# State products of the prompt in fp32r: three passes over high and low parts, two pairs of heads side by side, first in each block

## The chip, the core and the metric

The kernel runs on one core of one Trainium2 chip. The metric is the device time of one execution, in microseconds. A core has a matmul engine (PE, with its weight loads as PEld), a vector engine (DVE), a scalar engine (ACT), a general engine (POOL) and a queue engine (SP, written SPq in the profile), each of which runs its own list of instructions in order and waits on semaphores of the others. SP issues nearly all loads, POOL the stores of results.

## What is computed

One layer of a streaming trunk for two requests at once: a prompt of 256 frames, and 8 running streams of 16 frames, 384 tokens in all (`T`; `TP` = 256 is the prompt's part). A combined projection of 2048 inputs feeds a pooling branch, a state-space branch with 64 heads of 64 channels in 8 groups, and gates; a second norm, a squared-ReLU MLP and residual sums follow. What the change touches is the state at the end of the prompt, the term behind the plus here:

```python
    last = cum[:, -1]
    w_end = jnp.exp(last[:, None] - cum)
    h = h * jnp.exp(last)[..., None, None] + jnp.einsum('bsgn,bsgr,bsgrp->bgrpn', Bc, w_end, xdt)
```

For the prompt h begins at zero, so over all 256 tokens the final state of a head is a sum over tokens of B (128 columns, one B for the 8 heads of a group) times the decayed input of the head (64 columns). It is an output, `new_ssm_prompt`; nothing else of this layer reads it. Two heads make a pair of 128 columns; a group has four pairs, and a block of the kernel treats two.

The group's gated norm, which the prediction comes to, is

```python
    h = y.astype(jnp.float32) * jax.nn.silu(z.astype(jnp.float32))
    h = h * lax.rsqrt(jnp.mean(h * h, axis=-1, keepdims=True) + EPS)
```

with the mean over the 512 channels of a group.

## The kernel before

Every large product is done in three passes: an fp32 operand is split into a high part in the format fp32r (a copy on ACT, L77, named `wh`) and a low part (a subtraction on DVE, L78, named `wl`), and `mm3` (L161) adds high x high, high x low and low x high. A **unit** is half a weight column of the input projection, 8 x 3 = 24 matmuls of 128 x 128 by 128 x 384; two units (q 0 and q 1) give one projection. `flow` (L121) runs a list of units: it fetches weights four units ahead on SP, splits them three units ahead, runs the unit's matmuls, calls its post-processing, and then lets `work` drain deferred tasks.

Deferred tasks are closures in the deque `todo` with a cost written by hand. `later(cost, tag, f)` adds one at the end; `work(2.6)` after each unit takes tasks until their costs have used up the allowance, with a debt carried on; `need(tag)` takes all tasks up to that tag at once. The order in which instructions stand on ACT and DVE follows from this: nothing is reordered behind it.

The stretch from 480 to 1310 us holds eight groups, g = 0 to 7. Each runs the projections BT and CT (B and C of the group), x0 to x3 and z0 to z3, and up to g = 6 one gate. The x projections pass a short causal conv with SiLU (`conv_units`, L522 on; its task goes to the front of the deque); z has a SiLU (L563). Between them stand, by a list written out by hand:

- `block(old, new)` (L587) twice per group: after x2 with old = (g-1, 1) and new = (g, 0), and after z3 with old = (g, 0) and new = (g, 1). Per block and for `old`, PE makes Y (L598 on; the decayed attention-like product, from the tiles `E` and `xdt`), closes it with the contribution of the running streams (L627), and makes the state products `pp` (L631); for `new` it transposes x (L638) into `xdt` and `xdw` (the input times its decay to the end of the prompt), and in a group's first block also B (L643) and C x B (`cb`, L646). `pp` is copied on ACT to `pe` (L662) and stored by two POOL DMAs.
- A block queues, for `new`: `xhl` (high and low part of the running streams' part of `xdw`, L718 and L719, stored to `x_scr` by SP at L720), the exponentials of four heads in two `E` tiles with their powers (L762 to L771), the decay of the running states `hs` (L703, on DVE) and the masks on E (L782); and for `old` the gated products: y x silu(z) (L729), its square on ACT (L732, L735), the running sum `ssum` (L738), and after the fourth the sum's high part `sh` (ACT, L744) and low part `sl` (DVE, L745).
- `update` (L841): the state update of the running streams, 8 fp32r matmuls of 128 x 256, once after z1's first unit for (g, 0) and once within x0 of the next group.
- `norm_mm(g-1)` (L786): after z1's second unit, two matmuls with a matrix of ones, `bc_g`, that sum `sh` (L790) and `sl` (L791) of group g-1 over partitions. So there is one each in g = 1 to 7, ahead of z2's first unit, and a last one between the gates.

In PSUM, 2 banks hold the projections (`mmtile`) and 6 in rotation everything else (`sstile`).

Of the kernel before, what the change touches and what calls it, by code (L numbers as in the profile page):

```python
# [7 lines left out]
F32 = mybir.dt.float32  # L8
# [7 lines left out]
P = 128  # L16
# [20 lines left out]
def build(ctx, tc, io):  # L37
# [190 lines left out]
    rstd = small.tile([P, T], F32, name="rstd")  # L228
    cst2 = small.tile([P, C_END - C_MASK], F32, name="cst2")

# [70 lines left out]
    with tc.manual_schedule():  # L301
        v.memset(warm, 0.0)
        s.dma_start(gpre, io["vec"][:, V_GPRE : V_GPRE + 16])
        for kind, *a in sum(pieces, []):
            (xload if kind == "x" else oload)(*a)
        sy.dma_start(vec, io["vec"])
        sy.dma_start(pst, io["state_pool"])
        sy.dma_start(cst[:, :C_MASK], io["cst"][:, :C_MASK])
        sy.dma_start(cst2, io["cst"][:, C_MASK:])
# [21 lines left out]
    small.tile([P, 88], F32, name="pad_small")  # L331
    tok = small.tile([P, 11, NH], F32, name="tok")
    decb = small.tile([P, NH, NB], F32, name="decb")
    with tc.tile_pool(name="phc", bufs=1, reuse_waits="tile") as pc, tc.tile_pool(name="phc2", bufs=2, reuse_waits="tile") as pc2:
        bufs = []
        for i in range(2):
# [78 lines left out]
        def dt_phase(pb):  # L415
# [22 lines left out]
            v.tensor_scalar(dta, dt, nA, -1.0, ALU.mult, ALU.mult)  # L438
            v.tensor_tensor_scan(cum, cst2[:NH, C_SCAN - C_MASK : C_SCAN - C_MASK + T], dta, 0.0, ALU.mult, ALU.add)
            sy.dma_start(cum_scr, cum)  # L440
# [62 lines left out]
    s.activation(onesr, ones, AF.Copy)  # L503
    nrm = pd1.tile([P, 32], F32, name="nrm")
    v.tensor_scalar(nrm, vec[:, V_NRM : V_NRM + 32], -1.0 / 8192.0, None, ALU.mult)
    pd1.tile([P, 64], F32, name="pad_phd")
    seg = lambda a: a.rearrange("p (b t) -> p b t", b=24)
    ncv = [0]

# [38 lines left out]
    def gate_units(n):  # L548
        def post(ps):
            t = small.tile([P, T], F32, tag="gbt", name=f"gbt{n}", bufs=2)  # L550
# [27 lines left out]
    def make_Cm(g):  # L578
# [6 lines left out]
        )  # L585

    def block(old, new):  # L587
        Y = []
        if old:
            g, hf = old  # L590
            need(f"E{g}_{hf * 2}", f"E{g}_{hf * 2 + 1}")
            d = S[g]
            for j in (hf * 2, hf * 2 + 1):
                y = sstile(f"Y{g}_{j}")
                Y.append(y)
                for sb, e0, c0, n in ((0, 0, 0, TP), (1, TP, P, P), (2, T, TP, P)):
# [28 lines left out]
        if old:  # L625
            for y, j2 in zip(Y, range(2)):
                te.matmul(y[:, TP:T], d["yis"][hf][:, j2 * P : j2 * P + P], ident, start=False, stop=True, skip_group_check=True)  # L627
            pp = sstile(f"pp{g}_{hf}")
            for j2 in range(2):
                for b in range(2):  # L630
                    te.matmul(pp[:, j2 * P : j2 * P + P], d["xdw"][hf][:, j2, b, :], d["Bk"][:, b, :], start=b == 0, stop=b == 1)  # L631
        trx = []
# [79 lines left out]
    def state_tasks(g, hf):  # L712
        d = S[g]

        def parts():
            xhl = pd.tile([P, 2, 2, P], F32R, tag="xhl", name=f"xhl{g}_{hf}", bufs=1)
            x = d["xdw"][hf][:, :, 2, :]
            s.activation(xhl[:, 0], x, AF.Copy)  # L718
            v.tensor_tensor(xhl[:, 1], x, xhl[:, 0].bitcast(F32), ALU.subtract)  # L719
            sy.dma_start(x_scr[g * 2 + hf], xhl.bitcast(F32))  # L720

        later(0.5, f"xhl{g}_{hf}", parts)

# [62 lines left out]
    def norm_mm(g):  # L786
# [4 lines left out]
        te.matmul(bc, onesr, d["sl"], start=False, stop=True)  # L791
        ms = pd.tile([P, T], F32, tag="ms", name=f"ms_g{g}", bufs=1)
        y = pd.tile([P, T], F32, tag="ssum", name=f"nwy_g{g}", bufs=1)
# [109 lines left out]

    ab, ms_, held = [], [], {}
    AR = 7
# [36 lines left out]
    at(narrow)  # L942
    items += tail_[5:8]
    at(norm_mm, G - 1)
# [760 lines left out]
```

## Time and profile before

| | |
|---|---|
| Time, median of 3 runs (lowest to highest) | 2799.66 us (2799.36 to 2801.17) |
| The profiled execution: its own time | 2798.04 us |
| The profiled execution: span of the core | 2796.3 us |
| Granted PE clock, mean over the span | 0.999 |
| PE busy | 2783.0 us, 100% |
| DVE busy | 1766.5 us, 63% |
| ACT busy | 1323.6 us, 47% |
| POOL busy | 191.0 us, 7% |
| HBM | 412.35 MB read, 77.89 MB written, 175 GB/s |
| State products L631: PE busy, instructions | 17.0 us, 128 |
| Table loads on ACT at L540, L762 and L552 | 16, 16 and 8, 1283 ns each |

A row of a timeline reads: start in us from the span's start, duration in us, engine, line, operation, output <- inputs, shape, count; in brackets the engine's idle time before it and what ended it. Rows with a count over 1 stand for so many instructions in a row, with the time from the first's start to the last's end. A matmul's time is modelled and overlaps the next one's, so PE's durations don't add up; the distance from start to start does.

### The profile page before, as it was taken

How to read it: one execution, taken by the hardware profiler on the slowest of the kernel's cores; microseconds unless marked ns; L12 is line 12 of the kernel's file. 1: busy time of each engine (PE TensorE's matmuls, PEld its weight loads, DVE VectorE, ACT ScalarE, POOL GpSimd, SP SyncE). 2: the span in 40 equal slices, each digit the busy share in tenths (PEclk: the TensorE clock that was granted, in tenths of full speed). 3: DMA queues.
4: the chain of work that ended last, by engine and by line, in shares of the span. 5: the costliest groups of instructions: out<-in, count | busy, mean ns of one | idle time of the engine just before them, and what ended most of it. 6: DMA issues, size and time to landing. Idle time of an engine off the chain costs nothing.

```text
span 2796.3 us, 40260 instructions
## 1 busy us (share of the span) xinstructions
PE 2783.0 (100%) x15964; PEld 2653.5 (95%) x15964; DVE 1766.5 (63%) x2217; ACT 1323.6 (47%) x2076; POOL 191.0 (7%) x295
## 2 busy tenths in 40 slices
PE   9999999999999999999999999999999999999998
PEld 9999999999999999999999988999999999999997
DVE  8774334567767667677643334666767667676766
ACT  6443223555555555554422223545555555555553
POOL 0000000000000000001000000000111111111111
PEclk9999999999999999999999999999999999999999
DMA  6444445556556556555744454445666666666656
GB/s 223 135 133 138 140 137 175 183 178 215 193 182 211 196 184 206 201 183 185 263 156 157 147 203 133 155 166 184 179 160 166 162 163 162 178 176 186 183 127 246
DMA packets 161468, 492.89 MB, mean 176 GB/s; under 512 B 20032, under 2 KB 43392, under 8 KB 156416
## 3 DMA queue, kind: packets, MB, share of 16 engines
q1 hardware_dynamic: 133008, 406.07, 43.4%
q0 software_dynamic: 28128, 84.24, 12.7%
q8 instruction: 125, 2.05, 0.3%
q14 instruction: 63, 0.52, 0.1%
q10 hardware_dynamic: 144, 0.01, 0.0%
HBM read 412.35 MB, written 77.89 MB: 175 GB/s over the span
## 4 chain that ended last, share of the span: by engine, by line
PE 98%; DVE 1%; ACT 0%; SPq 0%; issue 0%; DMA 0%; DVEq 0%; ACTq 0%
PE pj_up L162 6%; PE pj_up L164 6%; PE pj_up L163 6%; PE pj_x L163 5%; PE pj_x L164 5%; PE pj_x L162 5%; PE wd L1405 3%; PE pj_sp L162 3%; PE pj_z L164 3%; PE wd L1407 3%; PE wd L1406 3%; PE pj_z L163 3%; PE pj_z L162 3%; PE pj_sp L163 3%; PE pj_sp L164 3%; PE t L1405 2%
## 5 line engine op out<-in xcount | busy, mean ns | idle before, releaser
L162 PE MATMUL pj_up<-x1h,wh_up 128*128 128x384 f32 x992 | 334.2, 337 | 0.0
L163 PE MATMUL pj_up<-x1l,wh_up 128*128 128x384 f32 x992 | 333.3, 336 | 0.0
L164 PE MATMUL pj_up<-x1h,wl_up 128*128 128x384 f32 x992 | 333.3, 336 | 0.0
L162 PE MATMUL pj_x<-xgh,wh_x 128*128 128x384 f32 x768 | 257.2, 335 | 0.0
L164 PE MATMUL pj_x<-xgh,wl_x 128*128 128x384 f32 x768 | 256.6, 334 | 0.0
L163 PE MATMUL pj_x<-xgl,wh_x 128*128 128x384 f32 x768 | 256.6, 334 | 0.0
L78 DVE TENSOR_TENSOR wl_wd<-raw,wh_wd 128x1024 fp32r<-128x1024 f32 x168 | 201.8, 1223 | 62.8 <-ACT wh_wd L77 61.2
L77 ACT ACTIVATE wh_wd<-raw 128x1024 fp32r<-128x1024 f32 x168 | 174.2, 1053 | 84.5 <-PE pj_up L163 42.1
L162 PEld LDWEIGHTS pj_up<-x1h,wh_up 128*128 128x128 f32 x992 | 186.5, 188 | 4.5
L163 PEld LDWEIGHTS pj_up<-x1l,wh_up 128*128 128x128 f32 x992 | 186.5, 188 | 4.5
L164 PEld LDWEIGHTS pj_up<-x1h,wl_up 128*128 128x128 f32 x992 | 186.5, 188 | 0.0
L164 PE MATMUL pj_z<-xgh,wl_z 128*128 128x384 f32 x512 | 171.1, 334 | 0.0
L162 PE MATMUL pj_z<-xgh,wh_z 128*128 128x384 f32 x512 | 171.1, 334 | 0.0
L163 PE MATMUL pj_z<-xgl,wh_z 128*128 128x384 f32 x512 | 171.1, 334 | 0.0
L164 PE MATMUL pj_sp<-abh,wl_sp 128*128 128x384 f32 x512 | 171.0, 334 | 0.0
L163 PE MATMUL pj_sp<-abl,wh_sp 128*128 128x384 f32 x512 | 171.0, 334 | 0.0
L162 PE MATMUL pj_sp<-abh,wh_sp 128*128 128x384 f32 x512 | 171.0, 334 | 0.0
L78 DVE TENSOR_TENSOR wl_sp<-w_sp,wh_sp 128x1024 fp32r<-128x1024 f32 x64 | 78.4, 1225 | 110.0 <-ACT wh_sp L77 110.0
L162 PEld LDWEIGHTS pj_x<-xgh,wh_x 128*128 128x128 f32 x768 | 144.2, 188 | 0.0
L163 PEld LDWEIGHTS pj_x<-xgl,wh_x 128*128 128x128 f32 x768 | 144.2, 188 | 0.0
L164 PEld LDWEIGHTS pj_x<-xgh,wl_x 128*128 128x128 f32 x768 | 144.2, 188 | 0.0
L78 DVE TENSOR_TENSOR wl_x<-w_x,wh_x 128x1024 fp32r<-128x1024 f32 x72 | 87.4, 1221 | 81.4 <-ACT wh_x L77 81.4
(388 smaller groups left out, 7085.2 us busy)
## 6 DMA issues: line engine op xcount, KB each, us to landing
w_up<-w_up SPq DMA_DIRECT2D x126, 512.0 KB, 4.5
raw<-w_down SPq DMA_DIRECT2D x112, 512.0 KB, 7.2
w_x<-w_in SPq DMA_DIRECT2D x96, 512.0 KB, 4.2
w_z<-w_in SPq DMA_DIRECT2D x64, 512.0 KB, 4.4
w_sp<-w_ssd SPq DMA_DIRECT2D x64, 512.0 KB, 4.7
acc_scr<-ev POOLq DMA_DIRECT2D x126, 256.0 KB, 4.4
w_ga<-w_in SPq DMA_DIRECT2D x32, 512.0 KB, 3.5
w_pp<-w_pp SPq DMA_DIRECT2D x32, 512.0 KB, 3.4
```

The source lines that it names most:

```text
L77: s.activation(h, w, AF.Copy)
L78: v.tensor_tensor(l, w, h.bitcast(F32), ALU.subtract)
L162: te.matmul(out, wh, xh, start=first, stop=False)
L163: te.matmul(out, wh, xl, start=False, stop=False)
L164: return te.matmul(out, wl, xh, start=False, stop=last)
L1405: te.matmul(o, ah, wh[:, c], start=first, stop=False)
L1406: te.matmul(o, ah, wl[:, c], start=False, stop=False)
L1407: te.matmul(o, al, wh[:, c], start=False, stop=fin)
```

## The change

- The prompt's state products use fp32r: per block six matmuls (three passes for each of two token blocks of 128) in place of eight fp32 instructions. The operands are exchanged: B is now stationary and `xdw` moves, both pairs of heads side by side, so 256 columns at a time. The result is the state transposed, and the host's reordering of the output follows.
- For this B is split into high and low part for all three token blocks (one ACT copy and one DVE subtraction of 128 x 384 per group), and `xhl` holds all three blocks of `xdw` (ACT and DVE 128 x 768 in place of 128 x 256). Its task is charged 1.0 instead of 0.5, and `x_scr` is written by two SP DMAs.
- A block with a successor makes the state products first, ahead of Y. Those of the very last block come after a gate unit in the tail, directly ahead of the last `norm_mm`.
- The copy out (`state_out`) goes through the buffer `gbt`, and one POOL DMA stores 256 columns.
- Around it, small tiles move: the scan's ones get a tile and a POOL load of their own, `nrm` moves to another pool, the tiles `ms` and `cacc` share a buffer.

```diff
+    def state(g, hf):
+        need(f"xhl{g}_{hf}")
+        d = S[g]
+        pp = sstile(f"pp{g}_{hf}")
+        for b in range(2):
+            bh, bl = (d["Bk"][:, i, b, :] for i in range(2))
+            xh, xl = (d["xhl"][0][:, i, :, b, :] for i in range(2))
+            mm3(pp[:, : 2 * P].rearrange("p (j q) -> p j q", j=2), bh, bl, xh, xl, b == 0, b == 1)
+        return pp
+
+    def state_out(g, hf, pp):
+        pe = small.tile([P, T], F32, tag="gbt", name=f"pe{g}_{hf}", bufs=1)[:, : 2 * P]
+        s.copy(pe, pp[:, : 2 * P])
+        gp.dma_start(io["new_ssm_p"][g * 2 + hf], pe)
...
             need(f"E{g}_{hf * 2}", f"E{g}_{hf * 2 + 1}")
             d = S[g]
+            if new:
+                pp = state(g, hf)
             for j in (hf * 2, hf * 2 + 1):
...
-            pp = sstile(f"pp{g}_{hf}")
-            for j2 in range(2):
-                for b in range(2):
-                    te.matmul(pp[:, j2 * P : j2 * P + P], d["xdw"][hf][:, j2, b, :], d["Bk"][:, b, :], start=b == 0, stop=b == 1)
...
-            pe = pd.tile([P, 2 * P], F32, tag="pe", name=f"pe{g}_{hf}", bufs=1)
-            s.copy(pe, pp[:, : 2 * P])
-            for j2 in range(2):
-                gp.dma_start(io["new_ssm_p"][g * 4 + hf * 2 + j2], pe[:, j2 * P : j2 * P + P])
+            if new:
+                state_out(g, hf, pp)
...
-                Bk = d2["Bk"] = pd.tile([P, 2, P], F32, tag="Bk", name=f"Bk{g2}", bufs=1)
-                s.copy(Bk.rearrange("p b n -> p (b n)"), trB[:, :TP])
-                Bhl = pd.tile([P, 2, P], F32R, tag="Bhl", name=f"Bhl{g2}", bufs=1)
-                s.activation(Bhl[:, 0, :], trB[:, TP:T], AF.Copy)
-                v.tensor_tensor(Bhl[:, 1, :], trB[:, TP:T], Bhl[:, 0, :].bitcast(F32), ALU.subtract)
-                sy.dma_start(b_scr[g2], Bhl.bitcast(F32))
+                Bk = d2["Bk"] = pd.tile([P, 2, 3, P], F32R, tag="Bk", name=f"Bk{g2}", bufs=1)
+                tb = trB[:, :T].rearrange("p (b n) -> p b n", b=3)
+                s.activation(Bk[:, 0], tb, AF.Copy)
+                v.tensor_tensor(Bk[:, 1], tb, Bk[:, 0].bitcast(F32), ALU.subtract)
+                sy.dma_start(b_scr[g2], Bk[:, :, 2, :].bitcast(F32))
...
-        def parts():
-            xhl = pd.tile([P, 2, 2, P], F32R, tag="xhl", name=f"xhl{g}_{hf}", bufs=1)
-            x = d["xdw"][hf][:, :, 2, :]
-            s.activation(xhl[:, 0], x, AF.Copy)
-            v.tensor_tensor(xhl[:, 1], x, xhl[:, 0].bitcast(F32), ALU.subtract)
-            sy.dma_start(x_scr[g * 2 + hf], xhl.bitcast(F32))
-
-        later(0.5, f"xhl{g}_{hf}", parts)
+        def parts(b):
+            if "xhl" not in d or d["xhl"][1] != hf:
+                d["xhl"] = pd.tile([P, 2, 2, 3, P], F32R, tag="xhl", name=f"xhl{g}_{hf}", bufs=1), hf
+            xhl = d["xhl"][0]
+            x = d["xdw"][hf][:, :, b, :]
+            s.activation(xhl[:, 0, :, b, :], x, AF.Copy)
+            v.tensor_tensor(xhl[:, 1, :, b, :], x, xhl[:, 0, :, b, :].bitcast(F32), ALU.subtract)
+            if b.stop == 3:
+                for i in range(2):
+                    sy.dma_start(x_scr[g * 2 + hf][:, i], xhl[:, i, :, 2, :].bitcast(F32))
+
+        if (g, hf) != (G - 1, 1):
+            later(1.0, f"xhl{g}_{hf}", lambda: parts(slice(0, 3)))
+            return
+        later(0.5, f"xhl{g}_{hf}", lambda: parts(slice(2, 3)))
+        held["parts"] = lambda: parts(slice(0, 2))
...
-    items += tail_[5:8]
+    items += tail_[5:7]
+    at(lambda: held["parts"]())
+    items += tail_[7:8]
+    at(lambda: state_out(G - 1, 1, state(G - 1, 1)))
     at(norm_mm, G - 1)
```

Three places of the instruction lists show what moves. The first is PE in the first block of group 1, from the last matmul of x2 on: state products `pp`, `Y`, the running streams' product `yi`, and the transposes `trx`. Before:

```order
L164 MATMUL pj_x_5586<-xgh_401,wl_x_1_5537 128x384
L598 MATMUL Y_2_5656<-E_2_5203,xdt_2_5160 64x256 x2
L598 MATMUL Y_2_5656<-E_2_5203,xdt_2_5160 64x128 x4
L598 MATMUL Y_3_5663<-E_3_5214,xdt_3_5163 64x256 x2
L598 MATMUL Y_3_5663<-E_3_5214,xdt_3_5163 64x128 x4
L618 MATMUL yi_0_5670<-hs_0_5166,Cm_5417 32x128 x16
L627 MATMUL Y_2_5656<-cst,yis_1_5151 128x128
L627 MATMUL Y_3_5663<-cst,yis_1_5151 128x128
L631 MATMUL pp_1_5689<-Bk_4704,xdw_1_5159 128x128 x4
L638 MATMUL trx_0_5694<-cst,xs_5501 128x128 x3
```

After:

```order
L164 MATMUL pj_x_5589<-xgh_401,wl_x_1_5540 128x384
L162 MATMUL pp_1_5659<-xhl_1_5201,Bk_4706 128x256
L163 MATMUL pp_1_5659<-xhl_1_5201,Bk_4706 128x256
L164 MATMUL pp_1_5659<-xhl_1_5201,Bk_4706 128x256
L162 MATMUL pp_1_5659<-xhl_1_5201,Bk_4706 128x256
L163 MATMUL pp_1_5659<-xhl_1_5201,Bk_4706 128x256
L164 MATMUL pp_1_5659<-xhl_1_5201,Bk_4706 128x256
L620 MATMUL Y_2_5666<-E_2_5206,xdt_2_5162 64x256 x2
L620 MATMUL Y_2_5666<-E_2_5206,xdt_2_5162 64x128 x4
L620 MATMUL Y_3_5673<-E_3_5217,xdt_3_5165 64x256 x2
```

The products moved ahead of Y, to the end of the unit before the block.

The second is ACT behind that block, from the powers of the second E tile (before) or the unit split that took their place (after), up to the split of z2's first unit; `xs` is the conv's SiLU and `ysq` a square of the gated norm. Before:

```order
L770 ACTIVATE E_1_5779<-E_1_5779 128x2x128
L771 ACTIVATE E_1_5779<-E_1_5779 128x2x256
L77 ACTIVATE wh_z_1_0_5818<-w_z_1_0_5733 128x1024
L526 COPY cbuf_4238<-cstate 128x8x3
L528 COPY cbuf_4238<-cbuf_4238 128x15x3
L531 ACTIVATE cacc_5825<-cbuf_4238,vec 128x384
L532 COPY cstate<-cbuf_4238 128x27
L540 ACT_TABLE_LOAD
L540 ACTIVATE xs_5831<-cacc_5825,vec 128x384
L77 ACTIVATE wh_z_1_1_5874<-w_z_1_1_5792 128x1024
L735 ACTIVATE ysq_2_5880<-zs_2_5034 128x384
L77 ACTIVATE wh_z_2_0_5908<-w_z_2_0_5847 128x1024
```

After:

```order
L77 ACTIVATE wh_z_1_0_5815<-w_z_1_0_5735 128x1024
L528 COPY cbuf_4241<-cstate 128x8x3
L530 COPY cbuf_4241<-cbuf_4241 128x15x3
L533 ACTIVATE cacc_5822<-cbuf_4241,vec 128x384
L534 COPY cstate<-cbuf_4241 128x27
L542 ACT_TABLE_LOAD
L542 ACTIVATE xs_5828<-cacc_5822,vec 128x384
L785 ACT_TABLE_LOAD
L785 ACTIVATE E_1_5782<-cbc_1_5510,tok 128x128
L787 ACTIVATE E_1_5782<-cbc_1_5510,tok 128x128 x3
L793 ACTIVATE E_1_5782<-E_1_5782 128x2x128
L77 ACTIVATE wh_z_1_1_5876<-w_z_1_1_5789 128x1024
```

The second head of E_1 and the powers moved behind the SiLU, with a table load of their own; in the whole list there are 70 table loads where there were 47.

The third is DVE in the same group, from the decay of hs (before) or the split that passed it (after) to the low part `sl`. Before:

```order
L703 TENSOR_TENSOR hs_0_5166<-hs_0_5166,decb 128x2048
L78 TENSOR_TENSOR wl_z_1_1_5875<-w_z_1_1_5792,wh_z_1_1_5874 128x1024
L738 TENSOR_TENSOR ssum_5292<-ssum_5292,ysq_1_5295 128x384
L729 TENSOR_TENSOR zs_2_5034<-zs_2_5034,xs_4660 128x384
L78 TENSOR_TENSOR wl_z_2_0_5909<-w_z_2_0_5847,wh_z_2_0_5908 128x1024
L562 TENSOR_TENSOR zs_0_5912<-pj_z_0_5849,rstd 128x384
L738 TENSOR_TENSOR ssum_5292<-ssum_5292,ysq_2_5880 128x384
L729 TENSOR_TENSOR zs_3_5102<-zs_3_5102,xs_4810 128x384
L738 TENSOR_TENSOR ssum_5292<-ssum_5292,ysq_3_5917 128x384
L745 TENSOR_TENSOR sl_5921<-ssum_5292,sh_5920 128x384
```

After:

```order
L78 TENSOR_TENSOR wl_z_1_1_5877<-w_z_1_1_5789,wh_z_1_1_5876 128x1024
L718 TENSOR_TENSOR hs_0_5168<-hs_0_5168,decb 128x2048
L78 TENSOR_TENSOR wl_z_2_0_5908<-w_z_2_0_5849,wh_z_2_0_5907 128x1024
L567 TENSOR_TENSOR zs_0_5911<-pj_z_0_5851,rstd 128x384
L761 TENSOR_TENSOR ssum_5295<-ssum_5295,ysq_1_5298 128x384
L752 TENSOR_TENSOR zs_2_5035<-zs_2_5035,xs_4662 128x384
L761 TENSOR_TENSOR ssum_5295<-ssum_5295,ysq_2_5916 128x384
L752 TENSOR_TENSOR zs_3_5103<-zs_3_5103,xs_4805 128x384
L761 TENSOR_TENSOR ssum_5295<-ssum_5295,ysq_3_5920 128x384
L768 TENSOR_TENSOR sl_5924<-ssum_5295,sh_5923 128x384
```

The decay moved behind the split wl_z_1_1, and the third gated product with the sum ahead of it behind the split wl_z_2_0 and zs_0. On PE, the matmuls `bc_g` that read sh and sl stand where they stood, between z1's second unit and z2's first.

More of the change, by code (lines that the diff above doesn't have):

```diff
@@ L228, in build @@
     rstd = small.tile([P, T], F32, name="rstd")
-    cst2 = small.tile([P, C_END - C_MASK], F32, name="cst2")
+    cst2 = small.tile([P, C_SCAN - C_MASK], F32, name="cst2")
     xg, xr = [None] * KD, [None] * KD
@@ L308, in build @@
         sy.dma_start(cst[:, :C_MASK], io["cst"][:, :C_MASK])
-        sy.dma_start(cst2, io["cst"][:, C_MASK:])
+        sy.dma_start(cst2, io["cst"][:, C_MASK:C_SCAN])
         f4 = [wfetch(win[5, q], f"p4_{q}") for q in range(2)]
@@ L329, in build @@
     pha.close()
-    small.tile([P, 88], F32, name="pad_small")
+    small.tile([P, 80], F32, name="pad_small")
+    nrm = small.tile([P, 32], F32, name="nrm")
     tok = small.tile([P, 11, NH], F32, name="tok")
@@ L334, in build @@
     with tc.tile_pool(name="phc", bufs=1, reuse_waits="tile") as pc, tc.tile_pool(name="phc2", bufs=2, reuse_waits="tile") as pc2:
+        scan = pc.tile([NH, T], F32, name="scan")
+        gp.dma_start(scan, io["cst"][:NH, C_SCAN : C_SCAN + T])
         bufs = []
@@ L438, in dt_phase @@
             v.tensor_scalar(dta, dt, nA, -1.0, ALU.mult, ALU.mult)
-            v.tensor_tensor_scan(cum, cst2[:NH, C_SCAN - C_MASK : C_SCAN - C_MASK + T], dta, 0.0, ALU.mult, ALU.add)
+            v.tensor_tensor_scan(cum, scan, dta, 0.0, ALU.mult, ALU.add)
             sy.dma_start(cum_scr, cum)
@@ L503, in build @@
     s.activation(onesr, ones, AF.Copy)
-    nrm = pd1.tile([P, 32], F32, name="nrm")
     v.tensor_scalar(nrm, vec[:, V_NRM : V_NRM + 32], -1.0 / 8192.0, None, ALU.mult)
-    pd1.tile([P, 64], F32, name="pad_phd")
+    pd1.tile([P, 96], F32, name="pad_phd")
     seg = lambda a: a.rearrange("p (b t) -> p b t", b=24)
-    ncv = [0]
+    ncv, held = [0], {}
     def proj_units(ui, name, post):
@@ L549, in post @@
         def post(ps):
-            t = small.tile([P, T], F32, tag="gbt", name=f"gbt{n}", bufs=2)
+            if "pe1" in held:
+                t = held["pe1"].tile([P, T], F32, tag="gbt", name=f"gbt{n}", bufs=2)
+            else:
+                t = small.tile([P, T], F32, tag="gbt", name=f"gbt{n}", bufs=1)
             v.tensor_tensor(t, ps, rstd, ALU.mult)
@@ L791, in norm_mm @@
         te.matmul(bc, onesr, d["sl"], start=False, stop=True)
-        ms = pd.tile([P, T], F32, tag="ms", name=f"ms_g{g}", bufs=1)
+        ms = pd.tile([P, T], F32, tag="cacc", name=f"ms_g{g}")
         y = pd.tile([P, T], F32, tag="ssum", name=f"nwy_g{g}", bufs=1)
@@ L902, in build @@
                 items += gate_units(gates.pop(0))
-    ab, ms_, held = [], [], {}
+    ab, ms_ = [], []
     AR = 7
```

5 lines of the change are left out of this document (3 added, 2 removed).

## The prediction

> **What bounds the kernel now.** I read the page first: its busy times, and the chain of work that ended last.
>
> ```profile
> span 2796.3 us, 40260 instructions
> PE 98%; DVE 1%; ACT 0%; SPq 0%; issue 0%; DMA 0%; DVEq 0%; ACTq 0%
> ```
>
> The chain is PE for 98%. A microsecond that another engine gains or loses therefore counts only where PE waits for it. Next I took the busy times in the stretch that holds nearly everything the change touches, the eight groups of the input projection (columns: us, then busy time of PE, PEld, DVE, ACT and POOL, then PE's clock, DMA share and GB/s).
>
> ```profile
> 480.00:1310.00 830.00, 830.00 (x5552) 814.26 (x5551) 586.57 (x821) 451.99 (x884) 46.49 (x85) 1.00 0.58 193
> ```
>
> PE is busy for all of the 830 us at clock 1.00; DVE is free for 243 us and ACT for 378. So the change has two ways to act: by the PE time of its matmuls, and by making PE wait where it now hardly does. Those close places show in the view of one line that lists who waited for it. For the last subtraction of a group's sum of squares (sl, L745), which feeds the second matmul of norm_mm, it says:
>
> ```profile
> L745 DVE TENSOR_TENSOR sl<-ssum,sh x8: 557/558/559, 626.5 to 1316.3; 128x384 fp32r<-128x384 f32 x8
>   PEld bc_g L791: 0.5, 2
> ```
>
> Two of the eight groups already wait for sl, 0.5 us together. The timeline shows how little is spare in group 1:
>
> ```profile
> 626.49 0.56 DVE L745 TENSOR_TENSOR sl<-ssum,sh 128x384 fp32r<-128x384 f32 x1 [0.59 <-ACT sh L744]
> 627.72 0.34 PE L791 MATMUL bc_g<-sl,onesr 128*128 128x384 f32 x1
> ```
>
> and, three groups on:
>
> ```profile
> 943.06 0.56 DVE L745 TENSOR_TENSOR sl<-ssum,sh 128x384 fp32r<-128x384 f32 x1 [0.59 <-ACT sh L744]
> 943.68 0.44 PE L791 MATMUL bc_g<-sl,onesr 128*128 128x384 f32 x1
> ```
>
> In the first, sl ends at 627.05, 0.67 before its matmul starts. In the other it ends at 943.62 and the matmul starts 0.06 later. PE runs its instructions in order, and behind L791 stand the 24 matmuls of the next z unit: whatever makes sl later by more than these margins stops PE.
>
> **The state products (PE).** Before, 8 fp32 matmul instructions a block; after, 6 in fp32r with 256 moving columns. The trace has no such product, but it has fp32r matmuls of that very shape, the state update's.
>
> ```profile
> 517.52 1.11 PE L841 MATMUL su<-xst,bst 128*128 128x256 f32 x8
> 518.47 0.34 PE L162 MATMUL pj_z<-xgh,wh_z 128*128 128x384 f32 x1
> ```
>
> And the old products, with what follows them:
>
> ```profile
> 542.86 1.06 PE L631 MATMUL pp<-Bk,xdw 128*128 128x128 f32 x8
> 543.75 0.82 PE L638 MATMUL trx<-cst,xs 128*128 128x128 f32 x6
> ```
>
> Counted from start to next start, the old products take 543.75 - 542.86 = 0.89 us. The eight updates take 0.95, 0.119 each, so six take 0.71: 0.18 saved a block, 16 blocks, **-2.9 us**. Bounds: the unit matmuls above, of 384 columns, start every 0.174, and six of them would be 1.04, +2.4 us in all; at the price of two thirds of that, 0.116, it is -3.1. I take the update's row, which has the shape. The place ahead of Y costs nothing: its parts (xhl) are half a group old, and the block's other matmuls only change places.
>
> **What the change adds on ACT and DVE.** Per block the split of xdw grows from 256 to 768 columns on both, and in every first block the split of B grows too. Here are ACT's rows of group 1, from that split on.
>
> ```profile
> 602.50 0.42 ACT L718 ACTIVATE xhl<-xdw 128x256 fp32r<-128x256 f32 x1
> 602.94 1.28 ACT L762 ACT_TABLE_LOAD   x1
> 604.24 0.40 ACT L762 ACTIVATE E<-cbc,tok 128x128 f32<-128x128 f32 x1
> ...
> 606.59 0.40 ACT L770 ACTIVATE E<-E 128x256 f32<-128x256 f32 x1
> ...
> 607.42 0.39 ACT L762 ACTIVATE E<-cbc,tok 128x128 f32<-128x128 f32 x1
> ...
> 610.59 1.05 ACT L77 ACTIVATE wh_z<-w_z 128x1024 fp32r<-128x1024 f32 x1
> ...
> 616.80 1.04 ACT L77 ACTIVATE wh_z<-w_z 128x1024 fp32r<-128x1024 f32 x1
> ```
>
> Between 0.42 at 256 and 1.05 at 1024 columns lies 0.84 at 768 (estimate): +0.42 a block on ACT. On DVE, whose rows below take 0.55 at 384 columns and 1.23 at 1024, 512 more make +0.53. Over 16 blocks that is 7 and 8 us against 378 and 243 free: nothing, if it were the amount alone. It is not, since the table of deferred work now charges this task 1.0 in place of 0.5. The allowance after each unit is 2.6, so the task behind it moves: the second head of the last E tile, which ran ahead of the conv's SiLU, now comes after it. There the table must be loaded again, and the weight split wh_z_1_1, the decay of hs and the gated tasks all stand in a new order. Now DVE's rows of the same stretch:
>
> ```profile
> 611.67 1.23 DVE L78 TENSOR_TENSOR wl_z<-w_z,wh_z 128x1024 fp32r<-128x1024 f32 x1 [6.94 <-ACT wh_z L77]
> 612.81 0.55 DVE L527 TENSOR_TENSOR cbuf<-pj_x,rstd 128x384 f32<-128x384 f32 x1
> ...
> 616.16 2.28 DVE L703 TENSOR_TENSOR hs<-hs,decb 128x2048 f32<-128x2048 f32 x1
> 618.36 1.22 DVE L78 TENSOR_TENSOR wl_z<-w_z,wh_z 128x1024 fp32r<-128x1024 f32 x1
> ...
> 622.06 1.23 DVE L78 TENSOR_TENSOR wl_z<-w_z,wh_z 128x1024 fp32r<-128x1024 f32 x1 [1.54 <-ACT wh_z L77]
> 623.20 0.55 DVE L562 TENSOR_TENSOR zs<-pj_z,rstd 128x384 f32<-128x384 f32 x1
> 623.67 0.55 DVE L738 TENSOR_TENSOR ssum<-ssum,ysq 128x384 f32<-128x384 f32 x1
> 624.13 0.55 DVE L729 TENSOR_TENSOR zs<-zs,xs 128x384 f32<-128x384 f32 x1
> ```
>
> Before, DVE ran the 2.2 us decay at 616.16, while ACT worked on the SiLU and the split; then one ssum and one gated product, and then it had 1.54 idle before the next split. After, the decay and those two stand behind a split that is itself later.
>
> **The new chain in group 1**, each step by the starts above:
> - ACT starts xhl at 602.50 as before (DVE's xdw comes first), 0.84: 603.34.
> - Table 1.30 (602.94 to 604.24), two heads 2.35 (to 606.59), powers 0.83 (to 607.42), third head half of 2.35: wh_z_1_0 at 609.01, against 610.59. Its DVE half follows 1.08 later (610.59 to 611.67) and takes 1.14: cbuf at 611.23.
> - From cbuf to the end of the SiLU 4.09 (612.81 to 616.80, and 0.10 that the next row overlaps it): 615.32.
> - New: table 1.30, the fourth head 1.17, powers 0.83: wh_z_1_1 at 618.62, against 616.80. On DVE its low half 619.70 to 620.84.
> - Decay 2.20, to 623.04. DVE has then been idle from about 614.6 to 619.7, the room in which this decay stood before.
> - wl_z_2_0 at 623.04 (before 622.06), zs_0 at 624.18, ssum 0.47, second gated product 0.46, ending 0.55 later: 625.66. ACT's square in between 0.60, as the 0.59 that DVE idles ahead of sl: 626.26. Sum 0.47, third product to 627.28, square 0.60, sum at 627.88, and 0.56 + 0.59 later sl starts: 629.03, ending at 629.59.
> - L791 could start at 627.72 - 0.18 = 627.54. **PE waits 2.05 us.**
>
> Of the seven groups with a successor I use this for the four odd ones. In the even ones the decay isn't all: wh_z_2_0 waits there for its weights. SP's rows in group 1, and so its order:
>
> ```profile
> 604.76 0.33 SPq L720 DMA_DIRECT2D x_scr<-xhl  x1
> ...
> 615.99 7.65 SPq L70 DMA_DIRECT2D w_z<-w_in  x4
> ```
>
> and, in group 2, the split of z2's first unit and the matmul on sl:
>
> ```profile
> 726.76 1.06 ACT L77 ACTIVATE wh_z<-w_z 128x1024 fp32r<-128x1024 f32 x1 [0.43 <-DMA w_z<-w_in]
> 732.98 0.36 PE L791 MATMUL bc_g<-sl,onesr 128*128 128x384 f32 x1
> ```
>
> SP's rows between those two are back to back, so what delays x_scr delays the fetch: the longer DVE splits (0.27 for the 256 more columns of B, 0.53 for xhl) and one more issue of 0.33, together 1.13. The split goes to 727.89, its low half starts 1.06 later, at 728.95, and from there to the end of sl it is 629.59 - 623.04 = 6.55: 735.50, where L791 could start at 732.98 - 0.18 = 732.80. **PE waits 2.70 us**, three times.
>
> Sum of the waits: 4 x 2.05 + 3 x 2.70 = **+16.3 us**. The eighth group's norm_mm stands among the gates:
>
> ```profile
> 1319.62 0.34 PE L791 MATMUL bc_g<-sl,onesr 128*128 128x384 f32 x1
> ```
>
> Its sl starts at 1316.3 by the row above and takes 0.56, so it has 2.76 us to spare, more than any delay worked out here, and I add nothing.
>
> Bounds of this term: if the chain on ACT costs nothing and only one split more lies ahead, sl ends at 622.06 + 6.55 = 628.61, a wait of 1.07 in each, 7.5 us. At 3.0 each (an E head and the powers not overlapped as I have them) it is 21.
>
> **Costed at nothing.** The second table loads: ACT's listing has 70 of them in place of 47, 23 x 1.28 = 29 us more of the 378 that are free; only those in the chain above count. The single 256-column POOL DMA of the new states in place of two, the reordered host output, and the scan's own tile: POOL is busy for 46 of 830 us. The last block's products, now behind a gate unit, have a whole unit (4.2 us) for their parts. With six PSUM banks in rotation, trB takes the bank of the state products rather than of Y, at most some 0.1 us in each group.
>
> **Sum.** -2.9 + 16.3 = +13.4 on the profiled execution's 2798.0: 2811.4. The median of the runs shown is 1.6 higher, so 2813.0 is what I expect of the changed kernel's median.
>
> **Rivals.**
> - *No wait arises: not slower.* It decides if the chain to sl is shorter by 2.1 us than I sum it, in the decay or in the two squares. For it: the margin is read from one execution, and SiLU and E may overlap better with DVE. Against it: the decay must pass wl_z_1_1 in the new order, and nothing in the rows above is faster than I used it. It gives -2.9: 2797, no change by measurement.
> - *Only the split counts:* the 1.07 above, +7.5 - 2.9: 2804.
> - *The clock falls after each wait.* In these 830 us it is 1.00 and PE is busy throughout, so no row shows what an idle of 2 to 2.7 us does. If PE then ran as long again at half speed, each wait would cost double: 2813 + 16 = 2829. The Trainium skill (TensorE: Matmul & The Clock Gate, on what the gate does) gives an idle window of about 3.4 us for the step down; by that these waits pass without one, and no run here shows it yet.
> - *The second table load costs more than its row,* through a drain on ACT that the row leaves out. At as much again, 1.3, in seven groups it is +9: 2822. The rows here go from 602.94 to 604.24 for a load and its successor, which leaves no room for such a drain. The Trainium skill (ScalarE: Activation LUTs, What ACT_TABLE_LOAD costs) speaks against the change: about 1283 ns for the load, which this trace has too, and 1380 for a drain with it, which this trace does not show.
>
> **How the numbers follow.** Forecast 0.72, no wait 0.13, split alone 0.07, clock 0.04, table 0.04. The forecast's own range: waits of 1.5 to 3.0 in seven groups, 10.5 to 21, less 2.9, which is 2807 to 2818. For 8 in 10 I go down to 2801, which takes in the split alone with the matmuls at their lower bound, and up to 2820 for the table's case in part; outside stay no wait, the clock and the rest of the table's case. About 0.2%, 5.6 us, is what a measurement of this kernel can tell from no change. Slower by more than that (over 2805.3): nearly all of the forecast, the clock and the table, 0.78. Within: most of no wait, the split alone and the forecast's low end, 0.18. Faster needs -5.6, twice what PE can save here: 0.04.
>
> **What would show it.** Right: a wait of 2 to 3 us of PE ended by sl in seven groups, more in every second one; the state products at 0.71 a block; 23 more table loads; DVE idle ahead of wl_z_1_1, with the decay behind it. Wrong: bc_g right behind its unit in all groups (no wait), or a matmul cost near 1.04. A wait at another place, above all ahead of a unit for its wl or at Y for E, would break the sum from the other side.

## The result, and the profile after

| | before | changed |
|---|---|---|
| Median, us | 2799.51 (n = 4) | 2828.26 (n = 4) |
| Lowest to highest, us | 2798.3 to 2801.17 | 2825.0 to 2829.13 |
| Ratio, 95% interval | | 1.0101 (1.0089 to 1.0113) |

The change makes the kernel slower by 1.0%, 28.7 us. The forecast was slower by 13.4, with 2820 as the upper end of its range: the direction was right, the size about half.

The page of the changed kernel, its span and its chain of waits:

```profile
span 2827.3 us, 40274 instructions
PE 70%; DVE 12%; issue 7%; ACT 7%; DMA 3%; SPq 1%; POOL 0%; DVEq 0%; ACTq 0%; POOLq 0%
```

Before, PE was 98% of that chain. Now DVE and ACT hold 19% of it, and "issue" another 7%. That share of 2827 us is far more than the sum of PE's waits, so it can't be read as lost time. It says that somewhere in the kernel the chain runs over DVE and ACT for long stretches. The two largest in the view of PE's waits (us in all, times, longest) are new:

```profile
PE bc_g L813 <- ACT sh L767: 13.8, 7, 2.5
PE trB L661 <- DVE yis L668: 7.2, 7, 1.0
```

The first is the predicted one, in all seven groups. The second is one that the prediction put at 0.1 us a group: the transposes of B wait for DVE's product `yis`. Why they need it, since they don't read it, the view doesn't say; a PSUM bank that `yis` frees would be a reason, but that isn't shown.

For group 1 the chain that was worked out step by step can be laid beside the timeline. ACT and DVE:

```profile
603.78 0.85 ACT L735 ACTIVATE xhl<-xdw 128x768 fp32r<-128x768 f32 x1 [0.86 <-DVE xdw L687]
...
616.61 1.28 ACT L785 ACT_TABLE_LOAD   x1
...
621.00 1.22 DVE L78 TENSOR_TENSOR wl_z<-w_z,wh_z 128x1024 fp32r<-128x1024 f32 x1 [5.04 <-ACT wh_z L77]
622.14 2.29 DVE L718 TENSOR_TENSOR hs<-hs,decb 128x2048 f32<-128x2048 f32 x1
624.34 1.22 DVE L78 TENSOR_TENSOR wl_z<-w_z,wh_z 128x1024 fp32r<-128x1024 f32 x1
...
630.38 0.56 DVE L768 TENSOR_TENSOR sl<-ssum,sh 128x384 fp32r<-128x384 f32 x1 [0.59 <-ACT sh L767]
```

The prediction had xhl at 602.50, the split at 619.70, the decay ending at 623.04 (here 624.34) and sl ending at 629.59 (here 630.94). Each is late by 1.28 to 1.35, and the first already is. From xhl to the end of sl it was 27.09 in the prediction and is 27.16 here. The chain was right; its starting point was not.

PE's rows at bc_g in groups 1, 4 and 7:

```profile
630.40 0.44 PE L813 MATMUL bc_g<-sh,onesr 128*128 128x384 f32 x1 [1.86 <-ACT sh L767]
...
958.91 0.45 PE L813 MATMUL bc_g<-sh,onesr 128*128 128x384 f32 x1 [1.85 <-ACT sh L767]
...
1286.51 0.69 PE L813 MATMUL bc_g<-sh,onesr 128*128 128x384 f32 x1 [2.48 <-ACT sh L767]
```

And the start of the transposes of B in two neighbouring groups, from which the length of a group is read:

```profile
929.42 0.55 PE L661 MATMUL trB<-cst,xs 128*128 128x128 f32 x3 [1.02 <-DVE yis L668]
...
1038.41 0.55 PE L661 MATMUL trB<-cst,xs 128*128 128x128 f32 x3 [1.03 <-DVE yis L668]
```

A group takes 108.99 us. Before, by the same row of its own timeline, it took 105.26 to 105.55 from group 1 on. Here are two of those rows, with the `yis` ahead of the first:

```profile
599.15 0.42 DVE L650 TENSOR_TENSOR yis<-yi,tok 128x256 f32<-128x256 f32 x1
600.41 0.49 PE L643 MATMUL trB<-cst,xs 128*128 128x128 f32 x3
705.67 0.49 PE L643 MATMUL trB<-cst,xs 128*128 128x128 f32 x3
```

There `yis` ended at 599.57, 0.84 ahead of trB. What stands between two groups in the chain of waits accounts for both PE waits. Here is a piece of that chain in group 4 (start, us, what):

```profile
943.86 0.63 DVE cacc L538
944.51 0.62 ACT xs L542
945.13 1.28 ACT L785
946.43 0.40 ACT E L785
946.83 0.88 ACT E L787 x3
947.92 0.62 ACT E L794
948.54 0.95 ACT wh_z L117
949.55 1.11 issue
950.66 0.52 DVE hs L718
951.18 1.11 issue
952.32 0.55 issue
952.86 1.22 DVE wl_z L78
```

PE is not in it, nor in any of the 195 longest pieces of the 145 us around it: the chain goes from conv to SiLU, table load, E, weight split, decay, next split, and on through the next group, all on ACT and DVE with one weight fetch in that stretch. A loop runs from group to group on these two engines, and it is 109.0 us long where PE's own work is about 105. PE's waits are what is left over, at whatever places PE meets the loop.

Not every group is so pure. In groups 1 to 3 the same view runs for some 17 to 22 us behind bc_g along PE's z units before it comes back to DVE, and in groups 1, 2, 3 and 6 it passes fetches of w_z ahead of bc_g. So the loop is ACT's and DVE's for most of its length, not for all of it, and PE can still lengthen it: group 1, with PE at half clock behind bc_g (below), takes 110.43.

**Where the 31.0 us between the two profiled spans are,** counted on PE from start to start in both timelines, over the seven groups: the z unit ahead of bc_g 15.0 (2.0 in five groups, 2.2 and 2.65 in the others: the wait), the transposes ahead of trB 8.4 (1.19 each, of which 1.03 is the wait), trB and the product behind it 2.4 (0.35 each), bc_g 3.7 (0.87 where it mostly took 0.36), half clock in the z units of groups 1 and 7 3.6, two waits for a split among the last gates 1.3. The state products, with the switch ahead of them (below), give 3.0 back. The sum is 31.4, 0.4 more than there is to place.

### The profile page after: what moved, and what is told of

It reads as the page before. It is cut to its first block, busy times and chain, and to the rows that moved or that the text cites. A ratio compares the mean times of both kernels' runs of the same rounds, so it can differ in the third digit from the quotient of the medians.

```text
span 2827.3 us, 40274 instructions
## 1 busy us (share of the span) xinstructions
PE 2791.5 (99%) x15932; PEld 2656.8 (94%) x15932; DVE 1779.0 (63%) x2218; ACT 1360.3 (48%) x2092; POOL 184.3 (7%) x280
## 3 DMA queue, kind: packets, MB, share of 16 engines
q8 instruction: 125, 2.05, 0.3%
## 4 chain that ended last, share of the span: by engine, by line
PE 70%; DVE 12%; issue 7%; ACT 7%; DMA 3%; SPq 1%; POOL 0%; DVEq 0%; ACTq 0%; POOLq 0%
PE pj_up L162 6%; PE pj_up L164 6%; PE pj_up L163 6%; PE wd L1431 3%; PE pj_sp L163 3%; PE wd L1433 3%; PE wd L1432 3%; PE pj_sp L164 3%; PE pj_sp L162 3%; DVE cacc L538 2%; PE t L1431 2%; PE t L1433 2%; PE t L1432 2%; DMA w_z<-w_in 2%; PE pj_pp L164 2%
```

## The experiments

Three theories came out of the profile. ORDER: the charge of 1.0 in the table of deferred work moved tasks, and that made the loop longer. Its rivals are AMOUNT (the wider splits fill the loop) and POSITION (products ahead of Y make trB wait for a bank).

| run | median, us | before, same chip | ratio, 95% interval |
|---|---|---|---|
| e1_cost_half | 2804.38 | 2799.49 | 1.0019 (1.0010 to 1.0028) |
| e2_old_place | 2826.99 | 2799.49 | 1.0102 (1.0088 to 1.0116) |
| e3_before_cost_one | 2825.71 | 2799.49 | 1.0096 (1.0082 to 1.0110) |
| e4_half_old_place | 2803.79 | 2799.49 | 1.0017 (1.0008 to 1.0026) |
| e5_parts_late | 2807.80 | 2799.72 | 1.0032 (1.0020 to 1.0043) |
| e6_half_one_pass | 2804.94 | 2799.72 | 1.0018 (1.0009 to 1.0027) |
| e7_before_half_products | 2799.40 | 2799.72 | 1.0000 (0.9991 to 1.0009) |
| e8_parts_on_pool | 2811.57 | 2799.30 | 1.0041 (1.0029 to 1.0054) |
| e9_decay_first | 2807.90 | 2799.30 | 1.0031 (1.0019 to 1.0043) |
| e10_half_decay_early | 2800.48 | 2800.04 | 1.0001 (0.9992 to 1.0010) |
| e11_before_decay_early | 2799.21 | 2800.04 | 0.9997 (0.9989 to 1.0006) |
| e12_norm_later | 2799.93 | 2799.20 | 1.0003 (0.9994 to 1.0012) |

### One number: the charge

In the changed kernel the charge goes back (e1), or the products go back to their place (e2), or both (e4); in the kernel before the charge alone goes up (e3).

```diff
-            later(1.0, f"xhl{g}_{hf}", lambda: parts(slice(0, 3)))
+            later(0.5, f"xhl{g}_{hf}", lambda: parts(slice(0, 3)))
```

> The changed kernel with one number put back: the task that splits xdw is charged 0.5 again, all else stays. ORDER theory (the charge of 1.0 moved an E head, the decay of hs and the gated products, so that the ACT and DVE chain of a group became longer than PE's 105.4 us): 47 table loads, groups of 105.2 to 105.5 us, waits for sh, sl and yis gone (under 0.2 us each), 2796 to 2800. AMOUNT theory (the wider splits lengthen the chain): waits stay, 2810 or more. POSITION theory (state products ahead of Y make the transposes of B wait 1 us for yis): that wait stays at about 1 us in seven groups, bc_g's goes, about 2804 to 2807.

```diff
-            if new:
-                pp = state(g, hf)
             for j in (hf * 2, hf * 2 + 1):
...
                 te.matmul(y[:, TP:T], d["yis"][hf][:, j2 * P : j2 * P + P], ident, start=False, stop=True, skip_group_check=True)
+            if new:
+                pp = state(g, hf)
```

> The changed kernel, charge 1.0, with the six state products put back to their old place behind the closing of Y. ORDER theory: the transposes of B come at the same time as before, since the work ahead of them in the block is the same sum, so both waits stay: 2824 to 2830. POSITION theory: the wait for yis (7.2 us together) goes: 2816 to 2821.

```diff
-        later(0.5, f"xhl{g}_{hf}", parts)
+        later(0.5 if (g, hf) == (G - 1, 1) else 1.0, f"xhl{g}_{hf}", parts)
```

> The kernel before with one number changed: its task that splits xdw (256 columns) is charged 1.0 in place of 0.5, but for the last block. ORDER theory: 70 table loads and most of the loss without any change of the products, 2815 to 2828 (somewhat less than the changed kernel, since each split is 0.4 us shorter on ACT and 0.5 on DVE). AMOUNT and POSITION theories: no order effect, 2798 to 2803.

> The changed kernel with charge 0.5 and the state products behind the closing of Y. ORDER theory: as with charge 0.5 alone, 2796 to 2800, and the products take 0.71 to 0.80 us a block in place of 0.89. POSITION theory: 1 us per group faster than with the products first.

In e3 nothing is computed differently, no product, no size, no store, only the order of tasks; and it loses 26.2 us where the change loses 28.7. The charge put back in the changed kernel (e1) wins 24 back. So ORDER carries most of the loss, but 26.2 overstates its part, since the two losses are made up differently. In e3 PE's clock fell to half behind bc_g in six of seven groups, in the changed kernel in two. In windows of 2 us behind bc_g of groups 4 and 5, both with a wait of 1.45 (columns as in the prediction: PE, PEld, DVE, ACT, POOL, PE's clock, DMA share, GB/s), e3 has:

```profile
960.00:962.00 2.00, 2.00 (x12) 2.00 (x13) 2.00 (x2) 1.21 (x2) 0.00 (x0) 1.00 0.00 0
1070.00:1072.00 2.00, 2.00 (x8) 2.00 (x7) 2.00 (x3) 0.00 (x0) 0.00 (x0) 0.50 0.27 53
```

Its z units behind bc_g lose about 8 us to this, against 3.6 in the changed kernel. Group 4 alone ran at full clock, and can be compared:

```profile
930.27 0.55 PE L643 MATMUL trB<-cst,xs 128*128 128x128 f32 x3
...
1038.35 0.55 PE L643 MATMUL trB<-cst,xs 128*128 128x128 f32 x3 [0.17 <-DVE yis L650]
```

That is 108.08, where the kernel before takes about 105.3 and the changed one 108.99. By this one group the order alone makes some 2.8 of the 3.7 us by which a group grew, and the other 0.9 comes with the changed work. By e1 it is 3.0, with 0.6 left. ORDER thus carries between three quarters and five sixths; the rest goes with AMOUNT. POSITION falls: with the products in their old place the time is the same, with either charge. The wait at trB does shrink there, to 5.5 us in e2, and is gone in e4, but the groups take 108.92 and 105.90, hardly less than with the products first.

What ORDER got wrong is the rest. It expected 2796 to 2800 for e1 and e4, and 2804.4 and 2803.8 were measured. Its groups, by trB:

```profile
918.96 0.55 PE L661 MATMUL trB<-cst,xs 128*128 128x128 f32 x3 [0.18 <-DVE yis L668]
...
1024.91 0.55 PE L661 MATMUL trB<-cst,xs 128*128 128x128 f32 x3 [0.18 <-DVE yis L668]
```

For e1 that is 105.95, and every group from group 3 on is within 0.02 of it, though PE's own work is shorter than before. With the order restored, something still holds the period 0.6 above that of the kernel before. The waits that show for it are tiny, 0.18 at trB and 0.15 at bc_g.

### Is PE the bound at all?

If a loop on ACT and DVE sets the period, matmuls taken away should win nothing. In e6 (from e1) five of the six state product matmuls of a block are gone, in e7 (from the kernel before) two of four.

```diff
-        for b in range(2):
-            bh, bl = (d["Bk"][:, i, b, :] for i in range(2))
-            xh, xl = (d["xhl"][0][:, i, :, b, :] for i in range(2))
-            mm3(pp[:, : 2 * P].rearrange("p (j q) -> p j q", j=2), bh, bl, xh, xl, b == 0, b == 1)
+        te.matmul(
+            pp[:, : 2 * P].rearrange("p (j q) -> p j q", j=2), d["Bk"][:, 0, 0, :], d["xhl"][0][:, 0, :, 0, :], start=True, stop=True
+        )
```

> The changed kernel with charge 0.5, with five of the six state product matmuls of each block left out (the prompt's state is wrong, all else is computed). LOOP theory: PE's group is 1.2 us shorter, but the chain on ACT and DVE sets the period, so the waits grow instead: 2801 to 2805, groups of 105.9. Rival (PE sets the time, and its own matmuls around the small waits are what costs): 16 x 0.6 less, 2793 to 2796.

```diff
             for j2 in range(2):
-                for b in range(2):
-                    te.matmul(pp[:, j2 * P : j2 * P + P], d["xdw"][hf][:, j2, b, :], d["Bk"][:, b, :], start=b == 0, stop=b == 1)
+                te.matmul(pp[:, j2 * P : j2 * P + P], d["xdw"][hf][:, j2, 0, :], d["Bk"][:, 0, :], start=True, stop=True)
```

> The kernel before with two of the four fp32 state product matmuls of each block left out (the sum over the second 128 tokens is missing). PE's group is 0.9 us shorter. If PE alone set the time: 16 x 0.45 = 7 less, 2792 to 2793. LOOP theory (the chain on ACT and DVE lies just under PE's 105.4): it gains at most 1 to 4 us, 2796 to 2799, with waits for sh, sl or yis in every group.

Both win nothing measurable: 2804.9 against 2804.4 with all products, and 2799.4 against 2799.7. The groups of e6:

```profile
918.70 0.55 PE L660 MATMUL trB<-cst,xs 128*128 128x128 f32 x3 [1.28 <-DVE yis L667]
...
1024.58 0.55 PE L660 MATMUL trB<-cst,xs 128*128 128x128 f32 x3 [1.27 <-DVE yis L667]
```

The group takes 105.88: the period stays (only group 6, with a wait of 1.12 at bc_g, takes 107.33), and the wait at trB grows from 0.18 to 1.28, by 1.1 of the 1.2 us that were taken from PE. In the kernel before, whose PE is never idle, the loop lies so close under PE's work that half the products can go for nothing: groups 5 and 6 of e7, without a wait at bc_g, take 105.02, only 0.24 less than the 105.26 of the kernel before, though 0.9 us of products is gone from each. Its 98% of PE in the chain of waits hid this: the chain names the engine that ended last, not by how little.

### Where the amount goes

The split of xdw is 512 columns wider. Could it be put where the loop does not pass? In e5 the prompt's columns become a task at the end of the block's list; in e8 POOL does them.

```diff
-            later(1.0, f"xhl{g}_{hf}", lambda: parts(slice(0, 3)))
-            return
         later(0.5, f"xhl{g}_{hf}", lambda: parts(slice(2, 3)))
         held["parts"] = lambda: parts(slice(0, 2))
...
             decay_masks(g2, h2)
+            later(0.0, f"xp{g2}_{h2}", held["parts"])
```

> The changed kernel with the split of xdw cut in two: the running streams' 256 columns first, charged 0.5 as in the kernel before, and the prompt's 512 columns as a task of its own at the end of the block's list, charged nothing. LOOP theory (the work of ACT and DVE in a group forms a chain that runs from group to group and takes 105.95 us with charge 0.5, 0.5 more than PE's own work; the 0.4 us of ACT and 0.5 us of DVE that the wider split puts into it make the difference): groups of 105.2 to 105.4, no wait for yis, 2795 to 2799, at or below the kernel before. Rival (the amount counts wherever it stands, DVE and ACT being full): as with charge 0.5, 2803 to 2805.

```diff
+                gp.tensor_copy(xhl[:, 0, :, b, :], x)
+                gp.tensor_tensor(xhl[:, 1, :, b, :], x, xhl[:, 0, :, b, :].bitcast(F32), ALU.subtract)
```

> The kernel of the run before with late parts, but the prompt's 512 columns of xdw are split by POOL (copy and subtraction) in place of ACT and DVE. ACT and DVE then have the kernel before's work but for B's split (0.27 us more on DVE a group). LOOP theory (the chain of ACT and DVE work from group to group sets the time, and any work on it counts wherever it stands): groups of 105.2 to 105.5, 2796 to 2800. Rival (the late parts cost by their place, or POOL's work slows DVE): 2803 to 2810.

Both are slower than e1, not faster. In e5 the time, 2807.8, lies above the 2803 to 2805 of the rival too: the amount counts at the end of the list as well, and here for more than in one piece. One reason is seen in the rows, where the two pieces take 0.62 and 0.42 on ACT against 0.85 for the whole; that this is all isn't shown. In e8, above its rival's range as well, the loss has a cause that the timeline shows. DVE's weight split and POOL's subtraction in group 1:

```profile
605.44 2.29 DVE L118 TENSOR_TENSOR wl_z<-w_z,wh_z 128x1024 fp32r<-128x1024 f32 x1
```

```profile
605.37 1.28 POOL L741 TENSOR_TENSOR xhl<-xdw,xhl 128x512 fp32r<-128x512 f32 x1
```

The split takes 1.22 in the other rows, here 2.29: 1.07 more, nearly all of the time that POOL was at work beside it. The same stands in the first block of all eight groups; in the second blocks the split beside POOL takes 0.41 more. The work was taken off DVE and came back as DVE's delay.

### Which of the moved tasks

In e9, with the charge at 1.0, only the decay of hs is queued ahead of the E tasks (and charged nothing). On ACT the late E head and its extra table loads stay, 70 of them.

```diff
             state_tasks(g2, h2)
-            decay_tasks(g2, h2)
             final = new == (G - 1, 1)
+            if not final:
+                decay_state(g2, h2)
+            decay_tasks(g2, h2)
...
-        later(2.3, f"dec{g}_{hf}", decay)
+        later(2.3 if (g, hf) == (G - 1, 1) else 0.0, f"dec{g}_{hf}", decay)
```

> The changed kernel, charge 1.0, with the decay of hs queued right behind the split of xdw and charged nothing: on ACT the second E head still comes after the SiLU with a table load of its own (70 loads), on DVE the decay and the gated products stand ahead of the late weight split again. If the decay and the gated products in their late place are what lengthens the chain: waits of bc_g gone, 2803 to 2812. If the E head and the table load ahead of the weight split are: 2818 to 2828, waits at bc_g or elsewhere.

2807.9: about 20 of the 28.7 us come back with all the table loads still there. So the larger part of ORDER is the decay and the gated products behind the late weight split, and the E head with its table load the smaller part. Since the charge of nothing also draws later tasks forward, the two can't be parted more finely by this run. Its waits are in other places:

```profile
PE pj_z L162 <- DVE zs L567: 3.4, 7, 0.5
PE trB L661 <- DVE yis L668: 3.0, 7, 0.5
```

### Can the loop be made shorter than PE's work?

The decay ahead of E, with an empty task that keeps its charge in its place, in the changed kernel with charge 0.5 (e10) and in the kernel before (e11).

```diff
             state_tasks(g2, h2)
+            decay_state(g2, h2)
             decay_tasks(g2, h2)
...
-            decay_state(g2, h2)
+            later(2.3, None, nothing)
...
-        later(2.3, f"dec{g}_{hf}", decay)
+        later(0.0, f"dec{g}_{hf}", decay)
```

> The changed kernel with charge 0.5 and the decay of hs moved ahead of the exponentials' tasks (it runs on DVE right behind the split of xdw, while ACT computes the exponentials), an empty task with its charge of 2.3 kept in its old place so that nothing else moves. LOOP theory: the chain from group to group loses up to 2.2 us in each block and falls below PE's work, so PE sets the period again with the cheaper products: groups of 105.2, no waits at trB, 2794 to 2798. Rival (the loop runs elsewhere, over weight fetches or the x projections, and the decay only fills a gap): 2802 to 2806.

> The kernel before with the same move of the decay. LOOP theory: its groups, 105.3 to 105.4, are PE's own work, so it gains little: 2797 to 2800; the difference to the run with the changed products is then what the products alone are worth, 1 to 3 us. Rival as above: 2799 to 2801.

e10 takes 2800.5: 4 less than e1, the wait at trB gone, and level with the kernel before, though not the 2794 to 2798 that was expected. Its groups are 105.02 where nothing waits and up to 105.90 where bc_g does:

```profile
PE bc_g L814 <- ACT sh L768: 1.1, 2, 0.9
...
PE bc_g L815 <- DVE sl L769: 0.6, 4, 0.2
```

e11, where PE waits nowhere in the groups, has them at 105.26 to 105.55. The cheaper products are thus worth 0.24 us a group against 105.26, some 2 us in all, where PE is really the bound. The last run moved norm_mm behind z2's first unit, to take the waits at bc_g away.

```diff
+        u = z_units(g, 2)
+        items += u[:1]
         if g:
             at(norm_mm, g - 1)
-        items += z_units(g, 2)
+        items += u[1:]
```

> The run with charge 0.5 and the early decay, and norm_mm moved behind z2's first unit, so that sh and sl have 4.2 us more. LOOP theory: the waits of bc_g there (four groups, 0.5 us each with what they slow) go and PE sets every group at 105.0: 2795 to 2798, 2 to 4 less than without the move. Rival (the chain moves on: the norm's work on DVE comes a unit later and collides with the z products or the next block): 2799 to 2804, with a new wait at z's banks or at Y.

It does, and the chain moves on, as the rival had it, with the wait back at trB:

```profile
PE trB L661 <- DVE yis L668: 2.3, 4, 1.1
```

2799.9, no change from e10. No version here beats the kernel before by more than its measurement can tell.

## Why the prediction was half right

- **What bounds the kernel.** "A microsecond that another engine gains or loses therefore counts only where PE waits for it" was read from a chain that is PE for 98%. The sentence is true, but the reading missed that ACT and DVE ran nearly level with PE: e7 takes 7 us of matmuls away and wins 0.3.
- **State products: right.** Forecast 0.71 a block. The six stand 0.12 apart and take 0.80 with a switch to fp32 behind them:

```profile
1032.28 0.28 PE L162 MATMUL pp<-xhl,Bk 128*128 128x256 f32 x1
...
1033.08 1.96 PE L620 MATMUL Y<-E,xdt 128*64 128x256 f32 x24
```

  The switch was there before as well, between the unit and Y (the x units took 20.91 up to Y, and take 20.81 up to pp). So 0.89 + 0.10 - 0.80 is 0.19 saved, forecast 0.18.
- **The order and the wait at bc_g: right,** place and size. 2.05 forecast for group 1, 2.0 measured (1.86 for sh, 0.15 for sl); the first six groups have 1.85 to 2.03, the seventh 2.48. Only that the wait for sh comes first was not said.
- **The fetch in even groups: wrong.** 2.70 was forecast for groups 2, 4 and 6, and they wait as long as the odd ones. The chain in group 4 passes wl_z behind the decay there, with no weight fetch in between. The late fetch itself is there: ACT waits for these weights in all seven groups, 0.7 to 2.9 us. But the decay on DVE ends later still and covers it. It shows through only in group 7, an odd one, and by 0.2 in group 3:

```profile
1279.36 1.06 ACT L77 ACTIVATE wh_z<-w_z 128x1024 fp32r<-128x1024 f32 x1 [2.92 <-DMA w_z<-w_in]
1280.45 1.23 DVE L78 TENSOR_TENSOR wl_z<-w_z,wh_z 128x1024 fp32r<-128x1024 f32 x1 [0.55 <-ACT wh_z L77]
```

  DVE stands idle there for 0.55, and that is nearly the whole of the 2.48 against 1.86. The excess forecast for the even groups, 3 x 0.65, was 2 us.
- **The step that failed** is "ACT starts xhl at 602.50 as before", and with it "at most some 0.1 us" for trB. What the change does to ACT and DVE in the second block of a group is still there when the next first block begins. It was 1.28 us at xhl in group 1; e3, with the order alone, has xhl at 603.62 there, 1.12 late, and e1, with the wider splits alone, at 603.58. The margin at trB, 0.84 behind the end of `yis` in the kernel before, was not read as that at bc_g was. The delay is seen as 1.0 us at trB in every group: 7.2 in the view of waits, 10.8 from start to start with what runs slower around it. Each group was costed as if it began on time; the loop from group to group was not looked for. Of the 16.3 us forecast ahead of bc_g 15.0 came. What the sum had at nothing is 10.8 at trB, 3.7 in bc_g's own matmuls behind their wait, 3.6 of half clock and 1.3 among the last gates.
- **The clock: the rival's mechanism occurred,** in two groups of seven. In windows of 2 us (us, PE, PEld, DVE, ACT, POOL, PE's clock, DMA share, GB/s), group 1 and group 2 behind their waits of 1.86:

```profile
632.00:634.00 2.00, 2.00 (x7) 2.00 (x7) 2.00 (x3) 0.24 (x1) 0.00 (x0) 0.50 0.00 0
742.00:744.00 2.00, 2.00 (x14) 2.00 (x13) 2.00 (x3) 0.67 (x1) 0.00 (x0) 1.00 0.03 8
```

  In group 1 the matmuls then stand 0.32 apart for some 3 us, in group 7 for some 6, and that cost about 4 us with bc_g's share, where 16 was the rival's price for all seven. That its 2829 lies beside the measured 2828.3 is chance: more than half of what the forecast lacked is at trB. The Trainium skill (TensorE: Matmul & The Clock Gate, What's actually happening) has an idle window of about 3.4 us, by which none of these waits would be seen. The runs show a drop behind waits of 1.9 and 2.5, and in e3 of 1.4.
- **The table load's drain** does not show: after the load at 616.61 the next activation starts at 617.91, 1.30 later, as priced.

## What to carry to other kernels

Before costing an edit on a bound engine, ask how far below it the next loop lies: take work away from the bound engine and see whether the time moves. A charge in a table of deferred work is an edit of order: the charge alone, in the kernel before, cost 26.2 us, and the change with the charge put back lost 5. An equal time is not yet an equal cause: some 8 of those 26.2 us were half clock, against 3.6 in the change. A delay in a loop body that repeats is to be followed once around, until it comes back to its own start, not priced once and multiplied.

## What the runs showed of the hardware

- POOL's elementwise work slows DVE: a subtraction of 128 x 512 on POOL (1.28 us) stretched a DVE subtraction of 128 x 1024 from 1.22 to 2.29. The Trainium skill (GPSIMD Engine Reference, Specifications) says that the two share their interface to the SBUF when a DVE instruction has two inputs there; this trace agrees.
- A short wait of PE costs more than itself. Behind 0.18 at trB, the three transposes took 0.57 to the next start where they take 0.33 without a wait. Behind 0.15 at bc_g its two matmuls took 0.83 to 0.87 in place of 0.35 (both in e1).
- The clock can fall behind an idle stretch of 1.86 us, and needn't: of six such waits between 1.85 and 2.03 in the changed kernel, one was followed by half the clock. In e3 it fell behind waits of 1.44, 1.45, 1.61, 2.05, 2.29 and 2.40, and not behind another of 1.45. What decides isn't shown.
